# Starting a down projection's accumulators from PSUM, a conv moved to SBUF, and one norm put first, in a two-layer decoder trunk

## The chip, the cores and the metric

One core of one Trainium2 chip runs the whole program. The metric is the device time of one execution in microseconds, as the median of several. The engines are TensorE (PE), VectorE (DVE), ScalarE (ACT), GpSimd (POOL) and SyncE (SP); each works through its own queue in order. SP and ACT issue plain DMA transfers, POOL issues transfers that add to their destination.

## The reference

Two layers over 1024 tokens of width 1024, all in float32. Cut to what matters here:

```python
for l in range(2):
    h = rms_norm(x, ln1_g[l])
    pa, pb, pc = split(h @ w_in[l])
    y = concat([mla(pa), gla(pb), rwkv7(pc)])          # 512 + 256 + 256 wide
    x = x + y @ w_out[l]
    h = rms_norm(x, ln2_g[l])
    u = causal_conv3(h @ w_up[l]) + conv_b[l]          # 2 x 2816 wide, depthwise, width 3
    gate, val = u[..., :2816], u[..., 2816:]
    x = x + (silu(gate) * val) @ w_down[l]
return rms_norm(x, final_g)
```

## The kernel before, in words

Every float32 operand of a large matmul is split into a high part `h` (float32r, by an ACT copy) and a low part `l` (the difference, by DVE or POOL), and a product is three matmuls (`mm3`, L97). The up and down projections use a seven-product scheme: each pair of operands is cut in four quarters, sums of quarters are formed on DVE and POOL, and products numbered 1 to 7 take the place of eight.

The program is written with a tile framework. It tracks dependencies, places tiles in buffers by tag and orders the instructions of each engine by priority with a simulated timeline, so the order on an engine is not just that of the source. Tiles with one tag share its buffers; a new tile waits until the old one's last reader is done. A background list `bg` of generators is stepped by `tick()` as matmuls are written, with a pace `clock["q"]`.

The stages that the change touches, in each layer:

- *w_out* (`wout_w`, `out_part`). The weight rows k = 0 to 7 are loaded raw (`wos`), split into `woh`, `wol`, and multiplied with token tile i of y. For k = 5, 6, 7 the raw rows go to tag `ws` of pool `wp`, which has two buffers; POOL makes `wol` for k of 4 and up (L1172). Token tile 0 needs k = 5 to 7 last.
- *The norm before the up projection* (`up_norm`). For each token tile i it squares, transposes, scales by ln2_g (L1304), subtracts earlier quarters (`less`, L1283) and makes the right-hand operands B21, B22, T1, T2, T3 of the seven products. Tile 7's generator runs in `late()`, three ticks behind the start of the up products, followed by `late_sums`, which makes T4 (L1334 on).
- *The up products* (`product`, `evac`, `taps`). Block j of 22 gives 128 gate and 128 value channels. `evac` moves the products out of PSUM; `taps` starts the conv with an ACT operation and adds two taps on DVE (L1469). For j of 3 and up the conv's result stands in a wide PSUM tile (`bigps`, two buffers); for j under 3 in SBUF. Gate times value goes to `fdr[j]` in memory.
- *The down products* (`down_load`, `down_split`, `down_product`). Eleven pairs q of blocks fall in three groups of 3, 4 and 4. For each group the seven products run in ORDER = (1, 2, 5, 6, 3, 7, 4), each in two halves u, 36 matmuls a product for the first group and 48 for the others. Products 1, 6, 7, 4 use a wide PSUM tile that goes on accumulating, 2, 5, 3 two narrow ones. After each, DVE subtracts the PSUM tile from the SBUF accumulator `acc[c, u]` of quarter c = INTO[p] (L1643 wide, L1646 narrow). The accumulators lie in slots that the up stage used.
- `seed(c)` loads the residual `xmid` into the accumulators by SP, 8 transfers of 512 KB a layer, during the last up block.
- `DSUM` (`sum_a` to `sum_d`) makes the operand sums. For the first group they are DVE additions; for the others part of them are accumulating transfers on POOL's queue (`plus`, L1577).

Of the kernel before, what the change touches and what calls it, by code (L numbers as in the profile page):

```python
# [61 lines left out]
def trunk(ctx: ExitStack, tc: tile.TileContext, A, out, offs):  # L62
# [241 lines left out]
    for l in range(DEPTH):  # L304
# [852 lines left out]
        def wout_w(k, ws=None):  # L1157
# [6 lines left out]
            ws = slot("m9", [128, D], F32, "wos") if k < 5 else wp.tile([128, D], F32, tag="ws", name="wos")  # L1164
            nc.sync.dma_start(out=ws, in_=A["w_out"][l][k * 128:(k + 1) * 128, :])
            if k < 4:
                g = col("mla_out_norm_g", k)
                act.activation(woh[k], ws, AF.Copy, scale=g)
                dve.scalar_tensor_tensor(wol[k], ws, g, woh[k].bitcast(F32), ALU.mult, ALU.subtract)
            else:  # L1170
                act.activation(woh[k], ws, AF.Copy)
                pool.tensor_tensor(wol[k], ws, woh[k].bitcast(F32), ALU.subtract)  # L1172
# [275 lines left out]
        def late():  # L1448
            for _ in range(LATE):
                yield  # L1450
            yield from norms[-1]
            yield from late_sums()
# [19 lines left out]
        H0, H1 = HALF  # L1472


        def evac(j, p):
# [12 lines left out]
            elif p == 3:  # L1488
# [3 lines left out]
                act.activation(a, taps(u, j, a if j < 3 else bigps()), AF.Silu)  # L1492
            else:
                u = tmp[j, "v"]
                act.activation(u[:, H0], ps, AF.Copy)
                b = taps(u, NF + j, lp.tile([128, T], F32, tag="raw", name="b", bufs=2) if j < 3 else bigps())
# [40 lines left out]
        draw, dent, acc, chain, homes = {}, {}, {}, {}, {}  # L1537
# [26 lines left out]
        def down_item(n=1):  # L1564
            while dtodo and (n or dtodo[0][1] in DSUM):
                q, p = dtodo.pop(0)
                if p in DSUM:
                    DSUM[p](draw[q], q)
                else:
                    down_split(q, p)  # L1570
                    n -= 1
# [46 lines left out]
        def seed(c):  # L1618
            for u in range(2):
                acc[c, u] = slot(ACC[c][u], [128, 2, 512], F32, "acc")  # L1620
                nc.sync.dma_start(out=acc[c, u], in_=xview(xmid, c, u))

        def down_product(js, p):
            for u in range(2):
# [16 lines left out]
                a = acc[INTO[p], u]  # L1641
                if wide:
                    dve.tensor_tensor(a, a, big.rearrange("p (a b) -> p a b", a=2), ALU.subtract)  # L1643
                else:
                    for o in range(2):
                        dve.tensor_tensor(a[:, o], a[:, o], ps[o], ALU.subtract)  # L1646
# [6 lines left out]
        for n, (j, p) in enumerate(seq):  # L1653
# [8 lines left out]
            if j == NF - 1:  # L1662
# [5 lines left out]
                if p == 3:  # L1668
                    seed(0)
                if p == 4:  # L1670
                    seed(3)
                    seed(1)
                    seed(2)
# [7 lines left out]
        for g, js in enumerate(groups):  # L1681
            for p in ORDER:
                down_product(js, p)
                if l + 1 < DEPTH:
# [70 lines left out]
```

## Time and profile before

| | us |
|---|---|
| median of 3 runs (2733.74 to 2743.07) | 2741.74 |
| the profiled execution | 2732.9 |
| its span, first to last instruction | 2731.1 |
| PE busy in the span | 2629.2 |
| DVE busy | 1697.6 |
| ACT busy | 1127.0 |
| POOL busy | 1032.0 |

The busy times are of one execution. PE's ends are modelled, so that a busy PE may still be a slow one; the granted clock says which. A row's wait names what came last before the instruction could start.

### The profile page before, as it was taken

Reading aid. Unit: us, or ns where it says so; the run is one execution under the profiler, and the core shown is the slowest. Engines: PE = TensorE matmul, PEld = TensorE weight load, DVE = VectorE, ACT = ScalarE, POOL = GpSimd, SP = SyncE. Lnnn points to the kernel's source line nnn. Section 1 sums busy time; section 2 is a strip of 40 time slices with the busy share of each in tenths; the row PEclk is TensorE's granted clock in tenths of the full one; section 3 lists DMA queues with packets and bytes.
Section 4 is the critical chain, followed back from the end, with each engine's and each line's share of the span. In section 5 each row is a group of like instructions: output and inputs, shape, how many; then the busy total and the mean of one; then the engine's idle time right before and its main releaser. Section 6 shows DMA issues by size and latency. Waiting matters only on the chain.

```text
span 2731.1 us, 35559 instructions
## 1 busy us (share of the span) xinstructions
PE 2629.2 (96%) x13586; PEld 2134.9 (78%) x13586; DVE 1697.6 (62%) x2418; ACT 1127.0 (41%) x1860; POOL 1032.0 (38%) x897
## 2 busy tenths in 40 slices
PE   8999999999999999899999999999998999998997
PEld 7668788878778888778786777888787788886786
DVE  3446565645876666876733565655469766668775
ACT  4222254444444554433352223445444444444333
POOL 4446332242554444211234553222325544441211
PEclk9999989999999999999999999899999999999999
DMA  4112221133232222754411122211342222227641
GB/s 129 31 29 64 58 64 41 41 116 124 77 100 70 93 79 68 247 145 126 114 37 32 31 70 72 56 30 58 113 137 64 83 88 77 90 68 272 155 115 62
DMA packets 246266, 240.89 MB, mean 88 GB/s; under 512 B 40312, under 2 KB 188240, under 8 KB 246096
## 3 DMA queue, kind: packets, MB, share of 16 engines
q1 hardware_dynamic: 215104, 211.70, 24.0%
q0 software_dynamic: 9984, 18.88, 3.9%
q10 hardware_dynamic: 21008, 8.04, 1.2%
q8 instruction: 107, 1.75, 0.3%
q14 instruction: 63, 0.52, 0.1%
HBM read 178.80 MB, written 53.48 MB: 85 GB/s over the span
## 4 chain that ended last, share of the span: by engine, by line
PE 79%; DVE 9%; DMA 3%; ACT 3%; issue 3%; POOL 2%; SPq 0%; POOLq 0%; DVEq 0%; ACTq 0%
PE psb L97 26%; PE psr L97 19%; PE psa L97 18%; PE psa L1146 2%; DMA R<-in_ffn_w_down 1%; PE psa L1135 1%; PE psr L896 1%; PE psr L862 1%; PE psr L807 1%; DVE Ttmp L699 1%; DVE Tb L701 1%; PE psa L503 1%; PE psr L900 1%; PE psr L838 1%; PE psr L494 1%
## 5 line engine op out<-in xcount | busy, mean ns | idle before, releaser
L97 PE MATMUL psb<-hh,wh 128*128 128x512 f32 (+2 forms) x704 | 267.2, 381 | 5.1 <-ACT acc L748 3.7
L97 PE MATMUL psb<-hl,wh 128*128 128x512 f32 (+2 forms) x704 | 270.7, 385 | 0.8 <-DVE hl L208 0.8
L97 PE MATMUL psb<-hh,wl 128*128 128x512 f32 (+2 forms) x704 | 269.5, 383 | 1.3 <-POOL wl L258 1.3
L97 PE MATMUL psr<-B,RG 128*128 128x512 f32 x1032 | 254.1, 391 | 1.0 <-ACT s_va L1481 0.5
L97 PE MATMUL psa<-T,RG 128*128 128x512 f32 x1008 | 247.4, 391 | 1.0 <-ACT RG L1276 1.0
L97 PEld LDWEIGHTS psr<-B,RG 128*128 128x128 f32 x1032 | 193.4, 188 | 44.7 <-ACT s_va L1481 1.5
L1277 POOL TENSOR_TENSOR RG<-S_m,RG 128x512 fp32r<-128x512 f32 x86 | 120.2, 1398 | 274.1 <-ACT RG L1276 239.3
L97 PEld LDWEIGHTS psa<-T,RG 128*128 128x128 f32 x1008 | 190.0, 189 | 42.7 <-ACT RG L1276 1.8
L1276 ACT ACTIVATE RG<-S_m 128x512 fp32r<-128x512 f32 x176 | 110.9, 630 | 225.3 <-PE psa L97 120.3
L97 PEld LDWEIGHTS psb<-hh,wh 128*128 128x128 f32 (+1 forms) x704 | 132.5, 189 | 35.0 <-issue 4.9
L97 PEld LDWEIGHTS psb<-hh,wl 128*128 128x128 f32 (+1 forms) x704 | 133.0, 189 | 34.3 <-issue 10.5
L97 PEld LDWEIGHTS psb<-hl,wh 128*128 128x128 f32 (+1 forms) x704 | 132.9, 189 | 29.0 <-issue 5.4
L97 PE MATMUL psr<-T,RG 128*128 128x512 f32 x528 | 137.7, 403 | 11.2 <-ACT T L1276 9.2
L1577 POOL DMA_DIRECT2D R<-fdr x48 | 42.5, 885 | 266.2 <-issue 56.3
L1469 DVE SCALAR_TENSOR_TENSOR psb<-uv,convc,psb 128x1023 f32<-128x1023 f32 x76 | 97.7, 1285 | 55.5 <-ACT psb L1467 54.5
L97 PEld LDWEIGHTS psr<-T,RG 128*128 128x128 f32 x528 | 102.0, 194 | 35.8 <-ACT T L1276 10.1
L1276 ACT ACTIVATE de<-R 128x1024 fp32r<-128x1024 f32 x67 | 68.7, 1051 | 145.4 <-PE psb L97 58.7
L258 POOL TENSOR_TENSOR wl<-ws,wh 128x1024 fp32r<-128x1024 f32 (+1 forms) x40 | 91.2, 2281 | 98.0 <-ACT wh L256 62.9
L97 PE MATMUL psb<-de 128*128 128x512 f32 x384 | 109.0, 400 | 15.2 <-DVE de L1277 8.1
L1469 DVE SCALAR_TENSOR_TENSOR psb<-ug,convc,psb 128x1023 f32<-128x1023 f32 x76 | 97.5, 1283 | 25.2 <-ACT psb L1467 24.2
L256 ACT ACTIVATE wh<-ws 128x1024 fp32r<-128x1024 f32 (+2 forms) x44 | 43.7, 994 | 147.7 <-PE psb L97 139.8
L254 POOL TENSOR_TENSOR ws<-ws,pcol 128x1024 f32<-128x1024 f32 x36 | 71.6, 1992 | 77.7 <-DMA ws<-in_w_in 72.7
(541 smaller groups left out, 6645.0 us busy)
## 6 DMA issues: line engine op xcount, KB each, us to landing
wu_m<-in_ffn_w_up SPq DMA_DIRECT2D x88, 512.0 KB
fdr<-acc SPq DMA_DIRECT2D x44, 512.0 KB
R<-fdr SPq DMA_DIRECT2D x88, 256.0 KB
R<-in_ffn_w_down SPq DMA_DIRECT2D x88, 256.0 KB
ws<-in_w_in SPq DMA_DIRECT2D x38, 512.0 KB
R<-fdr POOLq DMA_DIRECT2D x48, 256.0 KB, 4.7
y_m<-ydr SPq DMA_DIRECT2D x16, 512.0 KB
xmid<-x SPq DMA_DIRECT2D x16, 512.0 KB
```

Source lines behind the costliest of these rows:

```text
L97: pe.matmul(o, lhsT=l, rhs=r, start=first, stop=last, skip_group_check=on)
L254: eng.tensor_tensor(ws, ws, g.rearrange("p (k o) -> p k o", o=1).to_broadcast([128, K, M]), ALU.mult)
L256: act.activation(wh, ws, AF.Copy)
L258: eng.tensor_tensor(wl, ws, wh.bitcast(F32), ALU.subtract)
L494: pe.matmul(pa, lhsT=kt[:, tk], rhs=qbd.rearrange("p h t -> p (h t)"), start=True, stop=True)
L503: pe.matmul(pu[:, 0:256], lhsT=keT[r, i, :], rhs=vT[i // 4][r, i % 4, :], start=True, stop=True)
L699: dve.tensor_tensor(t3, Tb[:, 0:k, k:k + 1].to_broadcast([128, k, w]), Ub[:, k:k + 1, k + 1:32].to_broadcast([128, k, w]), ALU.mult)
L1146: pe.matmul(po[:, 0:128], lhsT=pT[:, j * 128:(j + 1) * 128], rhs=v[:, j, h * 128:(h + 1) * 128], start=(j == 0), stop=(j == i))
L1276: act.activation(d[0], s, AF.Copy)
L1277: eng.tensor_tensor(d[1], s, d[0].bitcast(F32), ALU.subtract)
L1469: dve.scalar_tensor_tensor(a[:, d:T], u[:, 0:T - d], conv[:, 2 - d, jj:jj + 1], a[:, d:T], ALU.mult, ALU.add)
L1577: pool.dma_start(out=o, in_=x, accum_op=ALU.add)
```

## The change

It has these parts. (1) For k = 7 of w_out the raw rows go to tag `raw` of pool `lp`, and for k = 5, 6, 7 DVE makes the low part instead of POOL. (2) Each step of tile 7's norm from its transposes on is traced with high priority; `late_sums` is not. (3) For the last up block (j = 21) the conv's two results stand in SBUF as for the first three. (4) `seed` is gone. The first product into each quarter is copied from PSUM to the accumulator by ACT with scale -1 (p = 1, 5, 6, 4 of the first group); after the last product of the first group into quarter c (p = 2, 3, 4, 7 for c = 0, 1, 2, 3) `residual(c)` adds `xmid` by two accumulating transfers on POOL's queue. (5) `sum_d` is ordered on DVE behind the latest accumulator subtraction.

```diff
--- before.py
+++ after.py
@@ -1,5 +1,5 @@
 import math
-from contextlib import ExitStack
+from contextlib import ExitStack, nullcontext
 
 import numpy as np
 
@@ -1161,7 +1161,12 @@
                 woh[k], wol[k] = (RG[:, 2 * k - 10 + n].rearrange("p a k c -> p (a k c)") for n in range(2))
             else:
                 woh[7], wol[7] = (wp.tile([128, D], F32R, tag="wl", name="wo7") for _ in range(2))
-            ws = slot("m9", [128, D], F32, "wos") if k < 5 else wp.tile([128, D], F32, tag="ws", name="wos")
+            if k < 5:
+                ws = slot("m9", [128, D], F32, "wos")
+            elif k < 7:
+                ws = wp.tile([128, D], F32, tag="ws", name="wos")
+            else:
+                ws = lp.tile([128, D], F32, tag="raw", name="wos", bufs=2)
             nc.sync.dma_start(out=ws, in_=A["w_out"][l][k * 128:(k + 1) * 128, :])
             if k < 4:
                 g = col("mla_out_norm_g", k)
@@ -1169,7 +1174,7 @@
                 dve.scalar_tensor_tensor(wol[k], ws, g, woh[k].bitcast(F32), ALU.mult, ALU.subtract)
             else:
                 act.activation(woh[k], ws, AF.Copy)
-                pool.tensor_tensor(wol[k], ws, woh[k].bitcast(F32), ALU.subtract)
+                (pool if k < 5 else dve).tensor_tensor(wol[k], ws, woh[k].bitcast(F32), ALU.subtract)
 
         yt_ = {}
 
@@ -1448,7 +1453,12 @@
         def late():
             for _ in range(LATE):
                 yield
-            yield from norms[-1]
+            chain = norms[-1]
+            while True:
+                with tc.high_priority():
+                    if next(chain, "end") == "end":
+                        break
+                yield
             yield from late_sums()
         bg[bg.index(norms[-1])] = late()
         clock["q"] = 1.1
@@ -1470,6 +1480,7 @@
             return a
 
         H0, H1 = HALF
+        WIDE = range(3, NF - 1)
 
 
         def evac(j, p):
@@ -1489,11 +1500,11 @@
                 u = tmp[j, "g"]
                 dve.tensor_tensor(u[:, H1], ps, s[:, 2], ALU.add)
                 a = tmp[j, "a"] = xr.tile([128, T], F32, tag="x", name="acc", bufs=2)
-                act.activation(a, taps(u, j, a if j < 3 else bigps()), AF.Silu)
+                act.activation(a, taps(u, j, bigps() if j in WIDE else a), AF.Silu)
             else:
                 u = tmp[j, "v"]
                 act.activation(u[:, H0], ps, AF.Copy)
-                b = taps(u, NF + j, lp.tile([128, T], F32, tag="raw", name="b", bufs=2) if j < 3 else bigps())
+                b = taps(u, NF + j, bigps() if j in WIDE else lp.tile([128, T], F32, tag="raw", name="b", bufs=2))
                 a = tmp[j, "a"]
                 dve.scalar_tensor_tensor(a[:, H0], a[:, H0], -1.0, b[:, H0], ALU.mult, ALU.mult)
                 dve.tensor_tensor(a[:, H1], a[:, H1], b[:, H1], ALU.mult)
@@ -1534,7 +1545,7 @@
         INTO = {1: 0, 2: 0, 6: 1, 3: 1, 5: 3, 7: 3, 4: 2}
         AT = ((0, 0), (0, 1), (4, 0), (4, 1))
         ACC = (("m1", "kb00"), ("va00", "va11"), ("m2", "m0"), ("kb10", "kb01"))
-        draw, dent, acc, chain, homes = {}, {}, {}, {}, {}
+        draw, dent, acc, chain, homes, last = {}, {}, {}, {}, {}, []
 
         def down_load(q, parts):
             h = q % len(HOME)
@@ -1565,7 +1576,8 @@
             while dtodo and (n or dtodo[0][1] in DSUM):
                 q, p = dtodo.pop(0)
                 if p in DSUM:
-                    DSUM[p](draw[q], q)
+                    with tc.issue_after(last[0].ins) if p == "d" and last else nullcontext():
+                        DSUM[p](draw[q], q)
                 else:
                     down_split(q, p)
                     n -= 1
@@ -1615,10 +1627,9 @@
             i0 += 2 * u
             return x[i0 * 128:(i0 + 2) * 128, HALF[n]].rearrange("(t p) c -> p t c", t=2)
 
-        def seed(c):
+        def residual(c):
             for u in range(2):
-                acc[c, u] = slot(ACC[c][u], [128, 2, 512], F32, "acc")
-                nc.sync.dma_start(out=acc[c, u], in_=xview(xmid, c, u))
+                plus(acc[c, u], xview(xmid, c, u))
 
         def down_product(js, p):
             for u in range(2):
@@ -1638,12 +1649,18 @@
                     for q in js:
                         h, w = dent[q, p]
                         mm3(ps[o], (h[:, 0, tk], w[:, 0, tk]), (h[:, 1], w[:, 1]), first and q == js[0], q == js[-1], not first)
-                a = acc[INTO[p], u]
+                c = INTO[p]
+                if (c, u) not in acc:
+                    a = acc[c, u] = slot(ACC[c][u], [128, 2, 512], F32, "acc")
+                    for o in range(1 if wide else 2):
+                        act.activation(*((a, big.rearrange("p (a b) -> p a b", a=2)) if wide else (a[:, o], ps[o])), AF.Copy, scale=-1.0)
+                    continue
+                a = acc[c, u]
                 if wide:
-                    dve.tensor_tensor(a, a, big.rearrange("p (a b) -> p a b", a=2), ALU.subtract)
+                    last[:] = [dve.tensor_tensor(a, a, big.rearrange("p (a b) -> p a b", a=2), ALU.subtract)]
                 else:
                     for o in range(2):
-                        dve.tensor_tensor(a[:, o], a[:, o], ps[o], ALU.subtract)
+                        last[:] = [dve.tensor_tensor(a[:, o], a[:, o], ps[o], ALU.subtract)]
             for q in js:
                 dent.pop((q, p))
             down_item(len(js))
@@ -1665,12 +1682,6 @@
                 if p == 5:
                     for q in groups[0]:
                         down_load(q, (2, 3, 6, 7))
-                if p == 3:
-                    seed(0)
-                if p == 4:
-                    seed(3)
-                    seed(1)
-                    seed(2)
                 if p not in (1, 2):
                     down_item()
         drain()
@@ -1681,6 +1692,9 @@
         for g, js in enumerate(groups):
             for p in ORDER:
                 down_product(js, p)
+                for c, done in enumerate((2, 3, 4, 7)):
+                    if (g, p) == (0, done):
+                        residual(c)
                 if l + 1 < DEPTH:
                     if (g, p) == (0, 7):
                         col2 = load_cols(l + 1, "m9")
```

## Rows read from the trace of the kernel before

**Rows 1.** The page: busy time, share and instructions of each engine.

```profile
PE 2629.2 (96%) x13586; PEld 2134.9 (78%) x13586; DVE 1697.6 (62%) x2418; ACT 1127.0 (41%) x1860; POOL 1032.0 (38%) x897
```

**Rows 2.** Windows: start:end, length, each engine's busy time, PEclk, DMA share, GB/s.

```profile
590.05:602.48 12.43, 8.69 (x25) 5.46 (x23) 2.49 (x3) 3.18 (x6) 5.78 (x6) 0.73 0.28 99
707.16:721.40 14.24, 8.50 (x26) 6.23 (x25) 13.32 (x17) 3.83 (x8) 8.74 (x6) 0.78 0.26 74
1130.52:1172.49 41.97, 29.17 (x103) 22.20 (x102) 40.93 (x50) 14.54 (x15) 5.96 (x5) 0.84 0.86 295
...
2487.84:2524.19 36.35, 27.38 (x96) 20.26 (x95) 36.04 (x45) 13.15 (x14) 5.12 (x4) 0.86 0.80 278
```

**Rows 3.** The chain that ended last, w_out: start us, us, what.

```profile
586.31 1.54 DMA ydr<-o
...
590.25 4.37 DMA wos<-in_w_out
...
594.71 1.06 ACT wo L1171
...
595.84 2.36 POOL wo L1172
...
623.15 11.04 PE psr L97 x48
```

**Rows 4.** Timeline of PE, entry to the up stage, layer 0.

```profile
703.09 1.95 PE L1301 MATMUL psb<-dg,x 128*128 128x128 f32 x16
...
714.69 0.53 PE L97 MATMUL psr<-T,RG 128*128 128x512 f32 x1 [4.61 <-ACT T L1276]
716.36 5.06 PE L97 MATMUL psr<-T,RG 128*128 128x512 f32 x11 [1.13 <-POOL T L1277]
```

**Rows 5.** Timeline of DVE, the same stretch.

```profile
708.56 1.21 DVE L1304 TENSOR_TENSOR raw<-psb,pcol 128x1024 f32<-128x1024 f32 x1
709.80 2.43 DVE L1283 TENSOR_TENSOR raw<-raw,B_kb 128x256 f32<-128x256 f32 x2
...
738.99 2.31 DVE L1277 TENSOR_TENSOR T_m<-ts,T_kb 128x1024 fp32r<-128x1024 f32 x1
```

**Rows 6.** Windows of two stretches in layer 0, columns as in group 2.

```profile
704.85:741.30 36.45, 30.71 (x124) 24.58 (x123) 33.45 (x38) 15.09 (x24) 19.03 (x12) 0.91 0.15 43
1121.43:1167.20 45.77, 32.92 (x129) 25.08 (x127) 45.27 (x54) 19.33 (x20) 7.52 (x5) 0.91 0.86 288
```

**Rows 7.** Timeline of PE, first down group, layer 0.

```profile
1143.70 0.80 PE L97 MATMUL psb<-de_kb 128*128 128x512 f32 x1 [4.41 <-ACT acc L1492]
...
1156.85 0.50 PE L97 MATMUL psa<-de_sg 128*128 128x512 f32 x1 [2.23 <-DVE acc_m L1646]
...
1167.26 1.22 PE L97 MATMUL psb<-de 128*128 128x512 f32 x2 [5.74 <-DVE de L1277]
```

**Rows 8.** Timeline of PE, first down group, layer 1.

```profile
2503.58 0.74 PE L97 MATMUL psb<-de 128*128 128x512 f32 x1 [4.10 <-DVE acc_m L1643]
2505.89 0.80 PE L97 MATMUL psb<-de_kb 128*128 128x512 f32 x1 [1.57 <-DVE acc L1499]
```

**Rows 9.** Timeline of DVE, first down group, layer 0.

```profile
1154.31 0.68 DVE L1602 TENSOR_TENSOR R<-R 128x512 f32<-128x512 f32 x1
...
1157.31 1.21 DVE L1643 TENSOR_TENSOR acc_kb<-acc_kb,psb 128x1024 f32<-128x1024 f32 x1
```

**Rows 10.** Taps of the conv by destination: ns min/median/max, first and last start us.

```profile
L1469 DVE SCALAR_TENSOR_TENSOR psb<-ug,convc,psb x76: 1271/1286/1290, 787.8 to 2492.7; 128x1023 f32<-128x1023 f32 x38, 128x1022 f32<-128x1022 f32 x38
...
L1469 DVE SCALAR_TENSOR_TENSOR acc<-ug,convc,acc x12: 1270/2032/2393, 735.5 to 2126.7; 128x1023 f32<-128x1023 f32 x6, 128x1022 f32<-128x1022 f32 x6
```

**Rows 11.** Timeline of SP's DMA queue: one of the residual's loads.

```profile
1134.58 0.37 SPq L1621 DMA_DIRECT2D acc_m<-xmid  x1
```

**Rows 12.** The accumulating transfers R<-fdr on POOL: issue, and time to landing.

```profile
L1577 POOL DMA_DIRECT2D R<-fdr x48: 863/874/1238, 1140.1 to 2654.5; - x48
...
DMA to landing us min/median/max: 3.3/4.6/8.2
```

## The prediction

> **What bounds the kernel now.** I read the page first, then the core's PE rows for idle stretches, then windows over those, then what each stretch waits for. TensorE is busy 2629.2 us of 2731.1 [rows 1], so a gain can only come from places where PE idles or runs at its lower clock, and an edit to another engine counts only where PE waits for it. The price of a matmul at full clock is 11.04 us / 48 = 0.23 us (48 in an unbroken run) [rows 3]. With it, a window's loss is its length less its matmuls times 0.23. The four windows of [rows 2] give: end of w_out's first tile 12.43 - 25 x 0.23 = 6.7 us; entry to the up stage 14.24 - 26 x 0.23 = 8.3; first down group of layer 0 41.97 - 103 x 0.23 = 18.3, of layer 1 36.35 - 96 x 0.23 = 14.3. The first two stretches stand again in layer 1 with the same waits and nearly the same loss. Ceiling: 2 x 6.7 + 2 x 8.3 + 18.3 + 14.3 = 62.6 us. In each the granted clock is below 1 (0.73, 0.78, 0.84, 0.86 [rows 2]): after a gap of some microseconds the next dozen matmuls run at the lower level, 1.2 GHz, so a gap costs more than its length.
>
> **w_out.** Before, the raw weights of k = 7 wait for k = 5's buffer, which POOL frees last: the load is issued at 590.25, takes 4.37, then ACT 1.06 and POOL 2.36, and only at 598.24 does PE run on [rows 3]. The change gives that load a buffer of pool lp and moves three subtractions to DVE. DVE does such a 128x1024 two-input operation in 1.21 (the like shape in [rows 9]) against POOL's 2.36, and is idle there. How early the load starts depends on what held lp's bytes in attention. Latest: attention's last output leaves at 586.31 + 1.54 = 587.85 [rows 3]; then load 592.2, ACT 593.3, DVE 594.5, and PE ends the tile some 3.2 us sooner than before. Earliest: the load is issued with its neighbours before attention ends, nothing is waited for, and the whole 6.7 comes back. I cannot see the address, so between the two I take 5 us a layer: **10 us** (6.4 to 13.4). The DMA queue gets no new transfer, only one moved forward.
>
> **Tile 7's norm.** PE gets tile 7's transposes at 703.09, done near 705, but DVE scales them only at 708.56, because splits and sums of lower need stand ahead; then it takes 2.43 for two subtractions, and PE waits 4.61 for ACT's T and 1.13 for POOL's [rows 4, 5]. With priority the scaling can start at 705, 3.5 us sooner, and POOL's two splits of the tile go ahead of the weight sums queued there, so T can stand when PE needs it (714.69 - 4.61 = 710.1, the end of the product before). But nothing is taken off DVE: it is busy 33.45 of the 36.45 us to 741.30 [rows 6], where it ends the second T4 half (738.99 + 2.31 [rows 5]), due at PE right behind. If PE comes 8 us sooner to products that need late_sums, it waits there instead. What can really be won is DVE's idle 3.0 us and the time by which operations beside POOL are stretched: that same T4 row is a 128x1024 subtraction of 2.31, which alone takes 1.21 [rows 9], so 1.1 there, and it is not the only one. Bounds 0 and 8.3; I take 4.5, near this sum (3.0 + 1.1, and a little), a layer: **9 us**. Work pushed back is weight splits and the gate addition, each under 1 us.
>
> **First down group.** Three things hold PE here: 4.41 for the last block's silu, which holds a wide PSUM buffer; 2.23 for the DVE evacuation of the second product, which must follow the first's on the same accumulator; 5.74 for a split that DVE does late [rows 7]. In layer 1 they are 4.10 for an evacuation and 1.57 for the last block's gate, and smaller ones [rows 8]. The change takes the conv to SBUF, so both wide buffers stand free when the last product ends (1130.52, where the window of [rows 2] begins) and products 1 and 2 can be interleaved. It takes p = 1, 5, 6, 4 off DVE: three wide pairs, 6 x 1.21, and four narrow ones of 0.68 (the 128x512 row of [rows 9]), so 10 us less of DVE in a stretch where it is busy 45.27 of 45.77 us [rows 6]. ACT pays at most 10 x 1.06 = 10.6 us (the 128x1024 row of [rows 3] for all ten), hidden: it is busy 14.54 of 41.97 us here [rows 2]. The order edge on sum_d (DVE work for product 7, not needed for another 40 us) keeps 3 x 2 x 0.68 = 4.1 us from standing ahead of evacuations and splits of products 2 and 6.
>
> The residual's eight loads of 512 KB are replaced per layer by eight accumulating transfers on POOL's queue. Of the old ones four were issued from 1134.58 [rows 11], among the loads that the group waits for; 2 MB at the 295 GB/s of that window [rows 2] is 7 us of transfer time which those loads no longer share. The new ones run later, after each quarter's last product of the group. No row has a 512 KB accumulate. A 256 KB one takes 0.87 of POOL and 4.6 to landing [rows 12]; from that to double (9.2) are my bounds, 6 my value. The accumulators are next touched a group later, some 58 us (7 products x 36 x 0.23), so I cost them at nothing; the cover is gone only if POOL's queue holds other work (slower rival).
>
> The gap of 4.41 and 2.23 with the slow matmuls behind the first (12 x 0.2 = 2.4) should go: 9 us; of the 5.74 + 2.6 behind the third, DVE's relief up to that point (two wide evacuations 2.4 and two sum_d pairs 2.7) takes about 5, of which I count 3, since the first splits still wait for loads. Layer 0: 12 of 18.3. Layer 1: 4.10 + 1.57 + 2.0 of slow clock = 7.7, and little of the rest: 8 of 14.3. Together **20 us**; bounds 8 (only the PSUM gaps and their clock in layer 0) and 30.
>
> Against this stands the SBUF conv itself. The taps of the gate half take 1.27 to 1.29 us from PSUM, 76 times, and 2.03 in the median, up to 2.39, from SBUF in the first three blocks [rows 10]. Four taps of the last block so cost DVE 0 to 4.4 us more. At the end of the block POOL has little left to do (5.96 us in the whole window [rows 2]), so I count 0.5, inside the 12 and 8 above. The Trainium skill, SBUF — State Buffer, "Who interferes with whom", says that a DVE instruction with two SBUF inputs contends with a GpSimd one that reads SBUF and that one with a single SBUF input does not; the rows of the two forms agree, and by that rule alone the taps would cost the price of a busy POOL.
>
> **The sum.** 10 + 9 + 20 = 39 us. The profiled execution took 2732.9, so 2693.9 in its state; it lies 8.8 under the median of the three runs (2741.74), near the fastest. Against the median: 2702.7. I say 2702.
>
> **Rivals.** (a) *DVE stays the bound and the gaps move.* For it: DVE over 90% busy in both stretches [rows 6]; T4 due right behind; and the value half's buffer b now comes from lp's pair, which the third entry of product 5 also uses, so a late conv holds that entry. Then the norm gives nothing, the down group only its lower bound, say 9, w_out stays: 10 + 9 = 19, 2723. Against: 10 us leave DVE. (b) *All three close*: w_out 13, norm 14, down 27 = 54, 2688. For it: in layer 0 and 1 alike the losses lie only in these places; against: T4. (c) *The change does not do what it says*: the instruction order is made from estimates of duration and not from the chip, so an order that puts p = 2 first again leaves the gaps; only w_out's lower bound, 6 us: 2736. (d) *Slower: POOL's queue.* A residual transfer waits for the quarter's last evacuation, and these spread over the whole group. Behind it on the same queue stand the accumulating transfers that make the next group's sums. The next group's product 5, which needs them first, is due 58 + 2 x 11 = 80 us after this group's start (11.04 us a product of four blocks [rows 3]); a residual that waits for the end of this group's product 7, at 6 x 8.3 = 50 us, leaves 30 for the four blocks' sums, which at 2 transfers of up to 9.2 us each, one after the other, take up to 74. PE then waits up to 44 us a layer. It decides from 39 / 2 = 20 us a layer; with 28 each, 2 x 28 - 39 = 17 slower: 2759. Against: POOL is busy only 5.96 of 41.97 us there [rows 2], and transfers that land in 4.6 us overlap.
>
> **How the numbers follow.** Forecast 0.52, own range 2690 to 2714; (a) 0.20; (b) 0.14; (c) 0.08; (d) 0.06. The time is the forecast's, 2702. The range goes to (b)'s end below, 2682, and past (a) to 2732 above; (c), (d) and the far edge of (b) are left out. This kernel's measurement tells about 0.5%, 13.7 us, from no change: under 2728 counts as faster. Forecast and (b) lie there, (a) mostly: 0.82. Within: (c) and a rest of (a), 0.12. Slower: (d), 0.06.
>
> **What would show it.** Right: no wait for k = 7 near 595, the load of k = 7 issued before 588; a wait for T under 2 us; psb products of the first down group starting within 1 us of the last up product, copies on ACT, no wait on an accumulator; residual transfers on POOL landing before the next group's first evacuation. Wrong: a new PE wait on T4 near 735, on `de` from lp's buffers, or on R in the second group; DVE still full to the split of product 6; or a clock under 1 in the same three places.

## The result, and the profile after

The changed kernel takes 2709.14 us in the median (2704.34 to 2710.13), the kernel before, timed beside it, 2741.97: ratio 0.9883, 95% interval 0.9861 to 0.9906, so 26 to 38 us less. The forecast was 2702. The profiled execution took 2708.75, its span 2707.0.

The page of the profile after: the engines' busy times, which answer to [rows 1].

```profile
PE 2620.6 (97%) x13586; PEld 2129.8 (79%) x13586; DVE 1693.5 (63%) x2404; ACT 1145.0 (42%) x1880; POOL 1040.7 (38%) x907
```

PE is 8.6 us less busy and the span 24.1 shorter. Where these went is read from five moments that PE's timeline has in every run: the first product of w_out in each layer, the first product on T in each layer, the first transpose of layer 1's entry, and the end.

| stage | before | after | difference | forecast |
|---|---|---|---|---|
| start to w_out, layer 0 | 578.81 | 579.53 | +0.72 | 0 |
| w_out to first T, layer 0 | 135.88 | 129.09 | -6.79 | w_out -5, norm -4.5 |
| T to the layer's end, layer 0 (the first transpose of layer 1's entry) | 651.11 | 642.91 | -8.20 | down -12 |
| attention, layer 1 | 567.94 | 573.78 | +5.84 | 0 |
| w_out to first T, layer 1 | 135.62 | 129.12 | -6.50 | w_out -5, norm -4.5 |
| T to the end, layer 1 | 661.74 | 652.57 | -9.17 | down -8 |

Windows of the kernel after over the places of [rows 2], and over the 30 us that follow layer 0's first down group (fourth line); columns as there.

```profile
590.77:602.48 11.71, 11.39 (x51) 8.95 (x50) 4.82 (x7) 4.01 (x7) 1.50 (x4) 1.00 0.37 131
701.08:715.31 14.23, 8.74 (x28) 6.37 (x27) 13.34 (x17) 4.16 (x9) 8.75 (x6) 0.76 0.27 74
1125.28:1170.00 44.72, 41.43 (x177) 32.73 (x177) 44.72 (x52) 26.53 (x30) 10.22 (x9) 1.00 0.91 267
1170.00:1200.00 30.00, 25.83 (x106) 20.48 (x105) 17.68 (x20) 8.92 (x9) 11.59 (x11) 0.94 0.95 216
2475.03:2520.00 44.97, 40.75 (x173) 32.08 (x173) 43.65 (x51) 25.62 (x28) 12.91 (x9) 1.00 0.89 254
```

By the rule length less matmuls times 0.23, the loss at the end of w_out's first tile is now 11.71 - 51 x 0.23 = 0 (6.7 before), at the entry to the up stage 14.23 - 28 x 0.23 = 7.8 (8.3), in layer 0's first down group 44.72 - 177 x 0.23 = 4.0 (18.3), in layer 1's 44.97 - 173 x 0.23 = 5.2 (14.3). But the fourth window loses 30.00 - 106 x 0.23 = 5.6, where the kernel before, in the same 30 us behind its group, had 131 matmuls and lost nothing (1172.49 to 1202.49): a part of what the group won is given back at once.

**w_out.** SP's queue, then DVE, then PE at the end of the first tile, layer 0:

```profile
583.93 0.43 SPq L1170 DMA_DIRECT2D wos<-in_w_out  x1
```

```profile
591.90 1.22 DVE L1177 TENSOR_TENSOR wo<-wos,wo 128x1024 fp32r<-128x1024 f32 x1
```

```profile
595.45 0.73 PE L97 MATMUL psr<-wo_m,yhl_sg 128*128 128x512 f32 x2 [0.32 <-DVE x L1433]
```

The load of k = 7 is issued at 583.93 (590.25 before), behind x's two loads and before attention's last output leaves ACT at 586.63; DVE takes 1.2 a subtraction. PE's only wait left is 0.32, none for weights. The chain of [rows 3] is gone.

**The norm.** PE and DVE at the entry to the up stage, to be laid beside [rows 4, 5]:

```profile
708.62 0.80 PE L97 MATMUL psr<-T,RG 128*128 128x512 f32 x1 [4.62 <-ACT T L1281]
710.29 4.52 PE L97 MATMUL psr<-T,RG 128*128 128x512 f32 x11 [0.87 <-POOL T L1282]
```

```profile
702.48 1.22 DVE L1309 TENSOR_TENSOR raw<-psb,pcol 128x1024 f32<-128x1024 f32 x1
703.73 2.43 DVE L1288 TENSOR_TENSOR raw<-raw,B_kb 128x256 f32<-128x256 f32 x2
```

The same waits for the same two instructions, 4.62 and 0.87 (4.61 and 1.13 before), behind the same subtractions at the same pace (2.43 for two). Nothing moved.

**The first down group.** PE, and DVE just before PE's last wait:

```profile
1125.12 0.61 PE L97 MATMUL psb<-de_m,de_m 128*128 128x512 f32 x2
...
1142.16 0.49 PE L97 MATMUL psa<-de_sg 128*128 128x512 f32 x1 [2.14 <-DVE acc_m L1663]
...
1158.67 0.74 PE L97 MATMUL psb<-de_m,de_m 128*128 128x512 f32 x2 [0.78 <-DVE de_m L1282]
...
1182.12 2.93 PE L97 MATMUL psb<-de 128*128 128x512 f32 x6 [4.17 <-DVE acc_kb L1660]
```

```profile
1174.11 0.69 DVE L1597 TENSOR_TENSOR R<-R 128x512 f32<-128x512 f32 x1 [2.40 <-DMA R<-in_ffn_w_down]
...
1179.10 0.69 DVE L1597 TENSOR_TENSOR R<-R 128x512 f32<-128x512 f32 x1 [1.91 <-DMA R<-in_ffn_w_down]
1179.71 1.22 DVE L1282 TENSOR_TENSOR de_va<-R,de_m 128x1024 fp32r<-128x1024 f32 x1
1180.85 1.21 DVE L1660 TENSOR_TENSOR acc_kb<-acc_kb,psb 128x1024 f32<-128x1024 f32 x1
```

The group's first products stand among the last up products from 1114.58 on and run on at 1125.12 without a wait; the 4.41 for silu is gone and the 5.74 has become 0.78, but the 2.23 for an evacuation by DVE stayed, at 2.14. In their place stands a wait that was not there: 4.17 us at the seventh product (p = 4) for the evacuation of the sixth (p = 7). DVE did that at 1180.85, because a sum of the next group (L1597), which itself waited 1.91 and before that 2.40 us for a load, stood ahead of it.

**Attention of layer 1**, which the change does not touch, took 5.84 us more. A stretch of 50 us, some 337 us behind the layer's entry in both traces, after first, then before:

```profile
1688.70:1738.70 50.00, 47.87 (x282) 39.09 (x282) 31.33 (x63) 22.66 (x46) 15.43 (x16) 0.73 0.27 71
```

```profile
1703.50:1753.50 50.00, 47.88 (x319) 40.32 (x319) 34.16 (x72) 26.16 (x56) 16.95 (x19) 0.83 0.27 72
```

PE is as busy, with 282 matmuls against 319; the granted clock was 0.73 against 0.83, 5 us in 50. Over the whole stage the time lost to the lower level (length times what the clock is short of 1, in 13 windows) is 17.3 us before and 22.2 after, and between 16.8 and 25.0 in the other runs below, with stage lengths from 566.2 to 576.2 that roughly follow it. A profile shows one execution of a program, and executions of one program differ in this too: the kernel before, timed eleven times more beside the e2 runs, had spans from 2728.5 to 2746.9 us, with a mean granted clock of 0.975 in the shortest and 0.968 in the longest. The profiled execution of before had 0.975, which fits its lying 8.8 under its median and the spans differing by less than the medians; that its dip in attention was shorter than in the others is not shown, since they have no trace. The medians of before beside the four groups of experiments are 2737.8 to 2738.9, under the 2741.97 here, so the change is likelier worth less than 32.8 us than more.

### The profile page after: what moved, and what is told of

It reads as the page before. It is cut to its first block, busy times and chain, and to the rows that moved or that the text cites. A ratio compares the mean times of both kernels' runs of the same rounds, so it can differ in the third digit from the quotient of the medians.

```text
span 2707.0 us, 35550 instructions
## 1 busy us (share of the span) xinstructions
PE 2620.6 (97%) x13586; PEld 2129.8 (79%) x13586; DVE 1693.5 (63%) x2404; ACT 1145.0 (42%) x1880; POOL 1040.7 (38%) x907
## 4 chain that ended last, share of the span: by engine, by line
PE 76%; DVE 10%; DMA 4%; issue 4%; ACT 3%; POOL 3%; SPq 0%; POOLq 0%; DVEq 0%; ACTq 0%
PE psb L97 24%; PE psr L97 19%; PE psa L97 17%; PE psa L1146 2%; DMA R<-in_ffn_w_down 2%; PE psa L1135 1%; DMA R<-fdr 1%; PE psr L896 1%; PE psr L862 1%; PE psr L807 1%; DVE Tb L701 1%; DVE Ttmp L699 1%; DVE RG L1282 1%; PE psa L503 1%; PE psr L900 1%
## 5 line engine op out<-in xcount | busy, mean ns | idle before, releaser
L97 PEld LDWEIGHTS psb<-hh,wl 128*128 128x128 f32 (+1 forms) x704 | 132.1, 188 | 34.4 <-issue 10.5
L1282 DVE TENSOR_TENSOR de<-R,de 128x1024 fp32r<-128x1024 f32 x67 | 86.2, 1303 | 43.9 <-ACT de L1281 43.9
```

The lines of the kernel that those rows point to most:

```text
L97: pe.matmul(o, lhsT=l, rhs=r, start=first, stop=last, skip_group_check=on)
L1282: eng.tensor_tensor(d[1], s, d[0].bitcast(F32), ALU.subtract)
```

## The experiments

Each ratio is against the kernel before, with its 95% interval. The stages of the profiled executions, in us (w0, w1: w_out to first T; d0, d1: T to the layer's end; a1: attention of layer 1). Each stage is of one execution. The part of d0 and d1 up to the last up product, which no edit but the norm's is aimed at, took 415.0 to 418.4 us in layer 0 and 416.4 to 420.6 in layer 1 over the other twelve rows, so a difference of under some 4 us in d0 or d1 is not told from this spread by itself:

| run | ratio | w0 | d0 | a1 | w1 | d1 |
|---|---|---|---|---|---|---|
| before | 1 | 135.88 | 651.11 | 567.94 | 135.62 | 661.74 |
| the change | 0.9883 (0.9861 to 0.9906) | 129.09 | 642.91 | 573.78 | 129.12 | 652.57 |
| e1_wout | 0.9966 (0.9954 to 0.9977) | 128.95 | 652.20 | 575.11 | 132.98 | 659.70 |
| e1_wbuf | 0.9979 (0.9967 to 0.9991) | 130.75 | 649.41 | 569.80 | 134.69 | 660.99 |
| e1_down | 0.9955 (0.9940 to 0.9970) | 135.45 | 650.11 | 575.40 | 136.36 | 652.39 |
| e1_seeds | 0.9937 (0.9921 to 0.9953) | 128.93 | 643.86 | 574.50 | 133.20 | 657.34 |
| e2_noconv | 0.9930 (0.9910 to 0.9950) | 129.06 | 649.01 | 572.40 | 133.30 | 656.87 |
| e2_suma | 0.9892 (0.9872 to 0.9912) | 129.20 | 648.57 | 576.23 | 129.02 | 650.70 |
| e2_nores | 0.9894 (0.9872 to 0.9915) | 129.25 | 643.88 | 575.81 | 129.00 | 650.13 |
| e2_norm | 0.9916 (0.9896 to 0.9936) | 123.95 | 653.18 | 573.47 | 127.54 | 657.94 |
| e3_wsp | 0.9962 (0.9950 to 0.9975) | 133.94 | 652.51 | 572.09 | 133.07 | 658.26 |
| e3_noedge | 0.9928 (0.9913 to 0.9944) | 129.19 | 646.55 | 575.41 | 133.29 | 654.74 |
| e3_combo | 0.9877 (0.9862 to 0.9892) | 129.21 | 642.53 | 566.24 | 129.01 | 652.76 |
| e4_sums | 0.9878 (0.9858 to 0.9897) | 126.48 | 639.97 | 568.59 | 130.75 | 652.76 |

### The w_out edits alone, and their buffer alone (e1_wout, e1_wbuf)

```diff
...
+            else:  # k = 7; in both runs
+                ws = lp.tile([128, D], F32, tag="raw", name="wos", bufs=2)
...
-                pool.tensor_tensor(wol[k], ws, woh[k].bitcast(F32), ALU.subtract)
+                (pool if k < 5 else dve).tensor_tensor(wol[k], ws, woh[k].bitcast(F32), ALU.subtract)  # e1_wout alone
```

> The kernel before with the two w_out edits alone (the lp buffer for k = 7, three subtractions on DVE). Theory: the anchors of the two traces (first w_out product to the wait for T) moved by 6.8 and 6.5 us, so the whole first-tile loss comes back: 13 us less than before, ratio 0.995, and in the trace no wait for k = 7. Rival, the prediction's value: 10 us, 0.9964, with some wait of 1 to 2 us left in each layer. Rival 2: the gain is eaten by the wait for T, which is DVE's and does not move: 0 to 4 us.

> The kernel before with the lp buffer for k = 7 alone; the three subtractions stay on POOL. Theory: the late load was most of the loss, but POOL's three subtractions (2.36 each from about 588.5) then end at 595.6, some 1.4 us after PE would want the last, and the second at 593.2, 1 us late: about 2 us a layer of waits stay, so a gain of 9 us, 0.9967. Rival: the buffer alone is worth all, 13 us, and moving the subtractions gives nothing. Rival 2: POOL is the real limit, and the buffer alone is worth under 4 us.

In layer 0 both came about as the theories have them: 6.9 us for the two edits, 5.1 for the buffer alone. In layer 1 they gave 2.6 and 0.9. There the instruction order of these two programs differs from that of the changed kernel: attention's last output leaves ACT later, and SP issues y's next load, which waits for it, ahead of the weights. ACT and SP of e1_wout, then ACT of the change, layer 1 (first w_out product at 1934.72 and 1925.31):

```profile
1944.75 0.37 ACT L1149 ACTIVATE o<-psa,sm 128x128 f32<-128x128 f32 x1 [3.94 <-PE psa L1146]
...
1950.17 1.06 ACT L1176 ACTIVATE wo<-wos 128x1024 fp32r<-128x1024 f32 x1 [1.71 <-DMA wos<-in_w_out]
```

```profile
1945.23 0.32 SPq L1184 DMA_DIRECT2D y_m<-ydr  x1
1945.60 0.42 SPq L1170 DMA_DIRECT2D wos<-in_w_out  x1
```

```profile
1932.42 0.37 ACT L1149 ACTIVATE o<-psa,sm 128x128 f32<-128x128 f32 x1 [1.42 <-PE psa L1146]
...
1936.30 1.05 ACT L1176 ACTIVATE wo<-wos 128x1024 fp32r<-128x1024 f32 x1
```

In e1_wout the last output (L1149) comes 10.0 us after the first w_out product, in the change 7.1, and the weights' load at 10.9 against 4.4. In all runs with both w_out edits and without the norm's, w1 goes with this: 129.0 to 129.1 where the last output comes at 7.1, 133.0 to 133.3 where it comes at 10.0 (e3_wsp, with 10.5, has 133.07).

### The load order on SP put right by hand (e3_wsp)

This is e1_wout with one thing more:

```diff
-        prep_load(1)
         x_load(1)
         for k in range(5, 8):
             wout_w(k)
+        with tc.issue_after(wos7[0].ins):   # the load of k = 7
+            prep_load(1)
```

> The kernel before with the two w_out edits and one thing more: on SP the load of y's second tile is put behind that of the last w_out weights in both layers. Theory: the w_out edits alone gave 6.9 us in layer 0 but 2.6 in layer 1, because there SP issued y's load first, which waits for attention's last output, and the weights behind it at 10.9 us after the first w_out product instead of 4.4; with the order fixed both layers give 6.7: 13 us less than before, ratio 0.995, and no wait for k = 7 in either. Rival: layer 1 stays at 2.6 for another reason (the loads of k = 5 and 6 come later there), and the ratio stays near 0.9966.

SP and ACT of this run, layer 1 (first w_out product at 1937.47):

```profile
1940.84 0.42 SPq L1170 DMA_DIRECT2D wos<-in_w_out  x1
1941.43 0.32 SPq L1184 DMA_DIRECT2D y_m<-ydr  x1
```

```profile
1947.98 0.37 ACT L1149 ACTIVATE o<-psa,sm 128x128 f32<-128x128 f32 x1 [4.42 <-PE psa L1146]
...
1950.66 1.04 ACT L1176 ACTIVATE wo<-wos 128x1024 fp32r<-128x1024 f32 x1
```

The weights now go out at 3.4 us and ACT copies k = 7 at 13.2 instead of 15.4, yet w1 stays at 133.07: the last output is still at 10.5, ACT's copies of k = 5 and 6 stand behind it, and in both layers y's second tile, loaded later, makes PE wait (1.65 and 1.11 us for `yhl_sg`); layer 0 lost 5.0 of its 6.9. The theory falls: the load order alone is not what layer 1 lacked. Which step of the program's order moves attention's end there was not tried out.

### The down group's edits alone (e1_down)

> The kernel before with the down group's edits and the last block's conv in SBUF; w_out as before. Theory: the parts add, and this one is worth 7.4 us in layer 0 and 9.3 in layer 1 by the anchors of the two traces: 17 us less than before, ratio 0.994; the wait of about 4 us at the seventh product of layer 0's first group stands here too, since its cause (a sum on DVE in front of an evacuation, waiting for a load) comes with these edits. Rival: the full 20 of the prediction or more, 0.9927, because the new wait came from w_out's shift and is gone here.

Layer 1 gave its 9.35 alone, layer 0 only 1.0, although its new wait was 2.78 and not 4.17. Of the 7.2 us by which its d0 lies above the change's, 1.7 stand in the up stage; the largest wait behind it is near the layer's end, 3.60 us for a split (about 0.5 in the change); e2_suma shows how such a wait comes. So the parts do not add: the ratios of e1_wout and e1_down multiply to 0.9921, the change has 0.9883.

### Which of the down edits carries it (e1_seeds, e2_noconv, e2_nores, e3_noedge)

e1_seeds takes the accumulators back to loads and every evacuation to DVE, and drops the order edge too; e2_noconv has `WIDE = range(3, NF)`, the last block's conv in PSUM again; e2_nores drops the two lines that call `residual(c)`; e3_noedge drops `tc.issue_after(last[0].ins)`.

> The changed kernel with the accumulators seeded by loads again and every evacuation of the first group back on DVE, no order edge on the sums; w_out edits and the last block's conv in SBUF stay. Theory: the SBUF conv frees PSUM, so the first product starts at once, but DVE must then evacuate it and is full, so PE waits for DVE instead: w_out 13 and about 5 of the 17 of the down group, 18 less than before, ratio 0.9934. Rival: the PSUM buffers were all of it: 13 + 15 or more, 0.990, and copies and transfers give nothing. Rival 2: the conv alone gives nothing, 13, 0.9953.

> The changed kernel with the last block's conv back in PSUM; ACT copies, later residual, order edge and w_out as in the change. Theory, from the run that kept this conv but put the evacuations back on DVE (there layer 0's first down group lost 0.9 us and layer 1's 4.8 against the change): the SBUF conv carries most of the down group's gain, 7.3 + 4.4 us, so without it 12 us are lost against the change, about 2721, ratio 0.993, with the wait of some 4 us for the last silu back at the entry of the first group in both layers. Rival: the copies by ACT carry it, since they free DVE; then under 5 us are lost, 2713, 0.990.

> The changed kernel without the residual: it leaves out the eight accumulating transfers a layer, so the FFN's output lacks its residual. Theory: these 4 MB share the DMA engines with the second group's loads (share 1.09 between 1170 and 1182), which is why DVE waited 2.40 and 1.91 us there; without them the loads land in about 5 us instead of 6.8, and the wait of 4.17 us falls under 2: 3 to 5 us less in layer 0's first group, little in layer 1. Rival: the loads are late because their buffers come free late, and the wait stays near 4: under 1 us of difference.

> The changed kernel without the order edge on the last sums (d); all else as in the change. Theory, from the prediction: three blocks' sums, 6 x 0.68 = 4.1 us of DVE, stand again ahead of evacuations and splits in the first group, and PE waits 2 to 4 us longer there in each layer: 5 us lost, 2714, ratio 0.990. Rival: DVE's order is not decided by these sums, since the copies have made room: under 2 us, 0.988 to 0.989.

Against the change (d0, d1): without the copies, transfers and edge (e1_seeds) 0.95 and 4.8 us are lost, without the SBUF conv 6.1 and 4.3, without the edge 3.6 and 2.2; without the residual 1.0 is lost and 2.4 won. Counted only from the last up product to the layer's end, which leaves the spread of the up stage out, the losses in layers 0 and 1 are 7.2 and 7.4 without the SBUF conv, 3.4 and 3.5 without the edge, -0.6 and 6.4 without copies, transfers and edge, 1.0 and -1.4 without the residual; the pieces overlap and do not add. The w1 of three of them is again 4 us longer, since the order at attention's end is the other one (e1_seeds, e2_noconv, e3_noedge). PE of e2_noconv, first down group of layer 0:

```profile
1135.64 0.79 PE L97 MATMUL psb<-de_kb 128*128 128x512 f32 x1 [4.45 <-ACT acc L1503]
```

The silu's wait is back with 4.45 us. In layer 1 no such wait returns and the 4.3 stand in several others, so there the theory had the size and not the place. In e3_noedge DVE ran sums for the last product ahead of the evacuations into acc_m (from 1147.18 on), and PE waited 3.64 us for acc_m instead of 2.14:

```profile
1142.43 0.67 DVE L1614 TENSOR_TENSOR R<-R 128x512 f32<-128x512 f32 x1
...
1143.63 0.67 DVE L1615 SCALAR_TENSOR_TENSOR R<-R 128x512 f32<-128x512 f32 x1
```

In e2_nores, which leaves out the residual, the wait at the seventh product stayed, 4.57, and DVE waited 2.95 and 2.11 us for the two loads, against 2.40 and 1.91. So the residual's transfers do not make these loads late; what does, the rival's buffers or another thing, was not tried. The 6.8 us in the expectation is not the loads' time: it is how long nine of POOL's own accumulating transfers took to land there (6.7 in e2_nores), and the trace does not tell when SP's loads land.

### The edge on the first sums too, then POOL's scaling moved (e2_suma, e3_combo)

```diff
-  with tc.issue_after(last[0].ins) if p == "d" and last else nullcontext():
+  with tc.issue_after(last[0].ins) if p in ("a", "d") and last else nullcontext():
-        prefetch()                       # e3_combo alone
+        prefetch(dve if l else None)
```

> The changed kernel with the order edge on the first sums of a block (a) as well as on the last (d), so that no sum of the next group that waits for a load stands ahead of the evacuation of products 3 and 6. Theory: the new wait of 4.17 us near 1182 is only the order on DVE; it goes, with the 2.9 us that the lower clock costs behind it, and layer 1's 0.85: 6 to 8 us under the change, about 2702, ratio 0.986. Rival: the sums are then late for the next group, and PE waits there for de: 2707 to 2712, 0.988 to 0.990.

> The changed kernel with the order edge on the first sums too, and with the next layer's first prefetched weights scaled and split on DVE (1.22 each) instead of POOL. Theory: with the edge alone, the wait of 4.17 us fell to 0.20, but near 1306 POOL's scaling ran beside DVE, two DVE splits took 4.05 us instead of 2.4 and four sums 3.90 instead of 2.6, and PE waited 5.37 us for the split; without POOL there that wait falls under 1.5, and with the clock behind it 5 us come back in layer 0: about 2700, ratio 0.986. Rival: the wait is DVE's own queue, and 1.22 more on DVE makes it longer: 2707 or above, 0.989.

PE, DVE and POOL of e2_suma; then POOL and DVE of the change at the same step:

```profile
1176.48 1.65 PE L97 MATMUL psb<-de 128*128 128x512 f32 x6 [0.20 <-DVE acc_kb L1660]
...
1312.56 1.22 PE L97 MATMUL psb<-de_m,de_m 128*128 128x512 f32 x2 [5.37 <-DVE de_m L1282]
```

```profile
1305.76 3.90 DVE L1615 SCALAR_TENSOR_TENSOR R<-R 128x512 f32<-128x512 f32 x4
1309.59 4.05 DVE L1282 TENSOR_TENSOR de_m<-R,de_m 128x1024 fp32r<-128x1024 f32 x2
```

```profile
1305.42 1.89 POOL L254 TENSOR_TENSOR ws<-ws,pcol 128x1024 f32<-128x1024 f32 x1 [1.93 <-DVE de_va L1282]
1309.42 1.99 POOL L254 TENSOR_TENSOR ws<-ws,pcol 128x1024 f32<-128x1024 f32 x1 [2.11 <-DMA ws<-in_w_in]
```

```profile
1309.64 7.03 POOL L254 TENSOR_TENSOR ws<-ws,pcol 128x1024 f32<-128x1024 f32 x1 [4.89 <-DMA ws<-in_w_in]
```

```profile
1309.61 1.22 DVE L1282 TENSOR_TENSOR de_m<-R,de_m 128x1024 fp32r<-128x1024 f32 x1
```

The wait of 4.17 became 0.20, as the theory had it: it was the order on DVE. But 130 us later a wait of 5.37 came, for a split as the rival has it: beside POOL's scaling of the next layer's weights (from 1309.42) two of DVE's splits took 4.05 us instead of 2.4. In the change it was the other way round: DVE ran at full pace and POOL's operation took 7.03 (the profile's POOL spans are rough). With one of these two scalings on DVE (e3_combo; the other stays on POOL and took 6.34) the wait fell to 2.25, not under 1.5 as forecast, and d0 from 648.57 to 642.53, yet no lower than the change's 642.91: its up stage took 1.5 us more than the change's, and behind it only 1.9 were won, since waits of 1.9 and 2.3 stand further on.

### Tile 7's norm truly first (e2_norm, e4_sums)

The programs with and without `tc.high_priority()` are the same, instruction for instruction, on all five engines; it changed nothing that could be timed. Why it moves nothing here was not looked into. So the order was made by edges; e4_sums stands on e3_combo and has its two edits as well:

```diff
-LATE = 3
+LATE = 0
+                with tc.issue_after(mark["t1"].ins):      # tile 7: low half's split behind T's
+                    split(at(B22), hi, pool)
+                with tc.issue_after(mark["lo"].ins) if j == 1 else nullcontext():
                     dve.tensor_tensor(tmp[j, "g"][:, H0], ps, s[:, 0], ALU.add)
+                with tc.issue_after(mark["t1"].ins) if j == 1 else nullcontext():  # the weight sums
                     eng.tensor_tensor(X[:, 0], v[:, 0:4], v[:, 4:8], ALU.add)
...
-    E1, E2, LD, EK, SJ, PD = pool, dve, (2, 5, 7, 4), 7, 1, (7, 4)   # e4_sums alone:
+    E1, E2, LD, EK, SJ, PD = pool, dve, (2, 5, 7, 4), 7, 3, (7, 4)   # blocks under SJ have their sums on DVE
```

> The changed kernel in which tile 7's norm really goes first: traced three ticks earlier, with order edges that put the second gate addition behind its four subtractions on DVE, and on POOL its low-half split behind T's and the weight sums of block 1 behind that. The arithmetic is the same. Theory: the two waits of 4.62 and 0.87 us before the first T product shrink to about 1.2 and 0.9, since the subtractions no longer run beside POOL (4.24 us for four, 1.5 alone): 3.4 us a layer and 1 to 2 of clock, so 7 to 10 under the change, about 2701, ratio 0.985. Rival, as in case (a) of the prediction: DVE is the bound of the stretch, the wait moves to T4 near 735, and under 2 us are gained: 2707 to 2709, 0.988.

> The kernel of the run before (order edge on the first sums, prefetched weights on DVE) with tile 7's norm first as in that earlier run, and with the eight weight sums of blocks 1 and 2 on DVE instead of POOL. Theory: in the run with the norm first, PE gained 5.1 us before T and lost 6.8 in the up stage, because the weight sums pushed behind T on POOL ran beside DVE from 706 on and stretched its operations (four subtractions 2.92 for two, a split pair 2.95, taps 2.3). On DVE these sums cost 8 x 0.68 = 5.4 us and some 14 us of stretch go; so the 5.1 us stay in each layer, the up stage goes back to 417 and 420, and the whole is some 8 us under the run before: about 2697, ratio 0.985. Rival: DVE is full there in either form, and 5.4 us more on it cost as much as the stretch did: T early, up stage at 422 or above, 2707 or more, 0.9885.

PE of e2_norm, then its DVE:

```profile
704.40 2.79 PE L97 MATMUL psr<-T,RG 128*128 128x512 f32 x11 [0.45 <-POOL T L1284]
708.57 0.50 PE L97 MATMUL psa<-T,RG 128*128 128x512 f32 x1 [1.38 <-ACT T L1283]
709.58 4.24 PE L97 MATMUL psa<-T,RG 128*128 128x512 f32 x11 [0.51 <-DVE T L1284]
...
730.69 3.50 PE L97 MATMUL psr<-T,RG 128*128 128x512 f32 x8 [2.58 <-DVE RG L1284]
```

```profile
700.89 0.76 DVE L1290 TENSOR_TENSOR raw<-raw,B_kb 128x256 f32<-128x256 f32 x2
...
711.68 2.92 DVE L1290 TENSOR_TENSOR raw<-raw,B_kb 128x256 f32<-128x256 f32 x2
...
718.67 2.95 DVE L1284 TENSOR_TENSOR T<-raw,T 128x256 fp32r<-128x256 f32 x2
...
726.65 2.32 DVE L1488 SCALAR_TENSOR_TENSOR acc<-ug,convc,acc 128x1023 f32<-128x1023 f32 x1
```

The subtractions take 0.75 a pair and T stands 5.1 us earlier. Then the weight sums, pushed behind T on POOL, run beside DVE: a pair of subtractions 2.92, a pair of splits 2.95, a tap 2.32, and PE waits 2.58 us for weights at 730.69. From w_out to the end of the up stage (its last product ends at 1127.01, at 1125.28 in the change) layer 0 lost 1.6 us. Of the 10.3 us that d0 is longer, 5.1 are T's standing earlier, 1.6 this loss, and 3.5 lie behind the up stage, where a wait of 3.27 near the layer's end is new, as in e2_suma. At 2715.42 us the run is slower than the rival's 2707 to 2709 too. The rival is right that DVE is the bound, though the wait came for weights and not for T4. PE and DVE of e4_sums:

```profile
706.53 0.50 PE L97 MATMUL psr<-T,RG 128*128 128x512 f32 x1 [2.36 <-ACT T L1283]
708.19 4.13 PE L97 MATMUL psr<-T,RG 128*128 128x512 f32 x11 [1.16 <-POOL T L1284]
```

```profile
714.65 0.76 DVE L1290 TENSOR_TENSOR raw<-raw,B_kb 128x256 f32<-128x256 f32 x2
...
718.87 0.75 DVE L1284 TENSOR_TENSOR T<-raw,T 128x256 fp32r<-128x256 f32 x2
```

With the sums on DVE its pairs are back at 0.75, and w_out to the up stage's end is 542.78 us against 547.39 in e2_norm and 545.75 in the change (layer 1: 548.66, 552.84, 549.72). So the stretch beside POOL was the price. In layer 1 the sum holds the other order at attention's end against it (the last output comes at 10.05), which this edit is not about. T itself comes 2.6 us sooner in layer 0 (126.48 against 129.09) and some 2.4 in layer 1 (130.75 against 133.0 to 133.3 in the runs with that order), and the up stage behind it, 416.30 and 417.91, lies within its spread. A part of the norm's term so exists, some 5 us of the 9, but only with the sums moved as well. Both forecasts for the whole, 2697 and 2707 or more, were missed: e4_sums and e3_combo, at 2704.09 and 2704.48 us in the median, are not told from the change by their intervals.

## Why the prediction was right, and which step failed

- **w_out, 10 forecast, 13.3 measured** (6.79 + 6.50). The mechanism was right; the size was chosen between two bounds because the buffer's address could not be seen, and it came out at the upper. (The lower bound's 3.2 a layer is 3.7 by its own rows, 598.2 less 594.5.) Alone the edits earned this in layer 0 only.
- **The norm, 9 forecast, nothing measured.** This is the step that failed: "With priority the scaling can start at 705". I took the priority block to move instructions; the program did not change, and the waits of 4.61 and 1.13 us for T stayed at 4.62 and 0.87, where the prediction's sign of being right was a wait under 2. Case (c), that the change does not do what it says, held for this part alone; I had thought of it for the down group's order. A real move alone would not have brought 4.5 a layer either, for case (a)'s reason, as e2_norm shows: T came 5.1 us sooner in layer 0 and the up stage gave 6.8 back. With the weight sums on DVE some 2.5 a layer were left.
- **The first down group, 20 forecast, 17.4 measured** (8.20 + 9.17). Layer 1 came as forecast. In layer 0 two of the three waits went and the loss fell from 18.3 to 4.0, more than I had counted; the third, 2.23, which should have gone too, stayed at 2.14, and 5.6 came back behind them as a wait that I had not named: a sum of the next group, waiting on its load, ahead of an evacuation on DVE's queue. I had counted what leaves DVE, not what stands in its order.
- **The conv in SBUF, 0.5 counted.** Seven of the eight taps of the last blocks took 1.27 to 1.28 us, as from PSUM; one in layer 1 took 3.42, beside a split on POOL, so that "at the end of the block POOL has little left to do" did not hold there. No wait of PE is put down to it. In layer 0 the SBUF conv is the largest piece of the group's gain (6.1 us of d0, or 7.2 from the last up product on); in layer 1 it is 4.3 or 7.4, with the copies, transfers and edge together near it at 4.8 or 6.4. DVE and POOL of the change:

```profile
2478.09 3.42 DVE L1479 SCALAR_TENSOR_TENSOR acc<-ug,convc,acc 128x1022 f32<-128x1022 f32 x1
```

```profile
2475.17 5.25 POOL L1282 TENSOR_TENSOR de_m<-R,de_m 128x1024 fp32r<-128x1024 f32 x1 [5.69 <-DMA R<-in_ffn_w_down]
```

- **Residual, at nothing.** The 512 KB transfers took 6.2, 8.6 and 9.3 us to land in the median of the three groups of accumulators, and up to 11.4, past my upper bound of 9.2 (8.2 to 10.0 for the one below); hidden all the same, so case (d) did not come. Issue on POOL and landing, acc_va:

```profile
L1589 POOL DMA_DIRECT2D acc_va<-xmid x4: 1197/1203/1228, 1176.3 to 2525.6; - x4
...
DMA to landing us min/median/max: 8.2/9.3/10.0
```

- **The sum.** 13.3 + 0 + 17.4 = 30.7 against 39; by the medians the change won 32.8. The forecast lay 7 us under the measured median, inside its range, since one term gave 3.3 more and two together 11.6 less than counted. That an empty term of 9 us still left the time inside is part luck: w_out came out at its upper bound, and the range reached 12 us above the forecast.

## What to carry to other kernels

Before a priority, a hint or an order edge is priced, compare the two programs' instruction orders: where they are the same, the price is nothing. Where an engine is full, count not only what leaves it but what stands ahead of the operation that PE waits for: here it was an instruction that itself waited for a load. And read a gain stage by stage: a stage that the edit does not touch took 566.2 to 576.2 us in these fourteen executions, as much of a difference as any one edit makes, and executions of one and the same program lie as far apart.

## What was not expected of the hardware

The time lost to the lower clock in layer 1's attention varied from 16.8 to 25.0 us over the fourteen profiled executions, in a stage that no edit is aimed at. Whether this goes with the program or only with the execution is not shown; the spans of the kernel before alone, 18 us apart with a mean clock of 0.975 and 0.968 at the two ends, say that the execution alone can do as much. And where DVE and POOL overlap, either may pay: the same scaling on POOL took 1.99 us while two DVE splits took 4.05, or 7.03 while DVE's splits took 1.22. In the first case POOL began 0.17 us ahead of DVE (1309.42 and 1309.59), in the second DVE 0.03 ahead of POOL (1309.61 and 1309.64). The Trainium skill, SBUF — State Buffer, "Who interferes with whom", says that the order of issue, and not the kind of operation, decides which of the two blocks; these rows agree, and on POOL's side no further than its rough spans allow. In the second case POOL's operation ended 1.85 us after DVE began its first instruction with a PSUM input (the evacuation at 1314.82), about its length in the first case: it reads as if POOL had been held over the whole row of six DVE instructions with two SBUF inputs before it.
